# A decoder trunk on one core: a fixed order of work up to the first pair of heads

## The chip, the core and the metric

The kernel runs on one core of a Trainium2 chip. A core has TensorE (matmuls, named PE in the profile, with PEld for the loading of weights into the array), VectorE (DVE), ScalarE (ACT), GpSimd (POOL) and SyncE (SP), whose queue only issues transfers here. Each engine works through its own queue in order, and semaphores hold an instruction until what it needs is there. The metric is the device time of one execution in microseconds (us).

## The reference

The input is 512 tokens of 1024 numbers, in 32 bit. Two layers follow each other: the first mixes tokens by attention with forget gates, the second by a short gated convolution. Each is followed by an MLP with squared ReLU and by a gated per-layer embedding, with an RMSNorm ahead of and behind every part. The change lies in the start of the attention:

```
hn = rmsnorm(x, g[0])
proj = hn @ w_in                      # q, k, v (1024 columns each) and 16 forget logits
q = proj[..., :D] * HEAD_DIM ** -0.5  # 16 heads of 64
log_f = log_sigmoid(proj[..., 3*D:] + b_f)
c = cumsum(log_f, axis=1)             # per head, along the tokens
s = q @ k^T + c[query] - c[key]       # masked: key <= query
o = softmax(s) @ v
```

## The kernel before

**Three products for one.** Every 32-bit operand is kept as a pair, a high part that TensorE takes without loss and the rest. `mm3` (lines 266 to 272) writes a product as three matmuls: high by high, low by high, high by low (lines 268 to 270). `split` (274) makes such a pair: ScalarE casts the high part (276), VectorE subtracts (277). `split_gained` (279) does so for weights that are multiplied by the first norm's gain as well (285 on ScalarE, 287 on VectorE, in halves of 256 columns).

**Weights.** All weights are listed in order of use as tiles of 128 x 512. `fetch(n)` (line 152) issues the loads of tiles up to n on SyncE's queue, into 14 raw buffers (`RAWS`); a raw buffer comes back when its tile is split. `prepare(n)` (175) splits tiles up to n, and fetches what isn't fetched. `wide` and `narrow` ask for one tile, and prepare `soon` tiles more than that one, 8 where nothing else is said (`SOON`). Tiles 0 to 19 are those of v and the forget logits in three blocks of columns (8, 8 and 4 tiles), tiles 20 to 51 those of q and k, four for each pair of heads. All split tiles and most intermediate results live in 70 pages of 128 x 512.

**The attention's start.** The v and logit columns are computed from x before it is normalised; the norm's factor is applied to the result, so TensorE can start at once. `halves` and `part` (472) do the first two blocks of columns, `values(t)` (482) the third, for four blocks of 128 tokens each. `keep_values` (498) applies the factor and splits into pairs. `logs` (419) turns the logits into logarithms. `sums_of_logs` (444) sums them along the tokens on TensorE (448), copies the sum to `c_T` (453) and writes it, less each block's start and negated, to `neg_c` in device memory (457, 461). `normed_x(n, ...)` (718) multiplies half n of x, with features along the partitions, by the factor (728) and splits it into `hT`. q and k are computed from `hT`: `project(i)` (521) does pair i of the heads, k first, then q, in eight steps of three matmuls each. It casts and scales the results, and copies k's parts to the other half of the partitions by four transfers (547). For pair 0 these are issued on ScalarE's queue, for the other pairs on SyncE's. `bias(h)` (550) broadcasts a head's row of `neg_c` to the 128 partitions, in four transfers (562), and GpSimd fills the masked corner of each (563). `scores` (568) is the product of q and k for one head and one block of queries, with the softmax behind it; `turn` transposes the weights and `mix` multiplies them by v.

**What sets the order.** A planner with its own estimate of times orders the instructions of each engine. Within the block that begins at line 733 the instructions of all five engines keep the order in which they are written among themselves; the planner may still place later instructions between them, where it thinks that the engine is free. That block ends at line 793, after `keep_values(1, 3)`. What follows, the last third of v, the two `bias` calls and pair 0, is ordered by the planner. From line 801 on, `main` is a stream of steps of the remaining pairs: eight steps of pair 1's k come first, and after them scores, transposes, products with v and steps of the stream alternate.

Of the kernel before, what the change touches and what calls it, by code (L numbers as in the profile page):

```python
# [8 lines left out]
F32 = mybir.dt.float32  # L9
# [6 lines left out]
P = 128  # L16
D = 1024
S = 512
# [3 lines left out]
KT = D // P  # L22
NB = S // P
# [6 lines left out]
RAWS = 14  # L30
# [38 lines left out]
def trunk(ctx: ExitStack, tc, x, xT, pT, g, gT, wv, wqk, bf, wo, wci, wcq, cw, wco, wup, wdn, wpp, wpg, out):  # L69
# [82 lines left out]
    def fetch(upto):  # L152
        while len(fetched) < min(upto, len(loads)):
            n = len(fetched)
            raw = raws.tile([P, S], F32, tag="raw", name=f"raw{n}")
            fetched.append(raw)
            src = loads[n]
            nc.sync.dma_start(raw[:, : src.shape[-1]], src)
# [16 lines left out]
    def prepare(upto, lows=None):  # L175
        while begun[0] < min(upto, len(order)):
            n = begun[0]
            begun[0] += 1
            key, at = order[n]
            for of in (key[:3], key[:2]):  # L180
                if of in recipes:
                    derive(of)
            hi, lo = page(f"wh{n}", F32R), page(f"wl{n}", F32R)
            if isinstance(at, tuple):
                raw, w = derived.pop(key), S
                eng = nc.gpsimd if (key[0] == "dn" and key[2] > 0) or key[-1] in ON_POOL else nc.vector
            else:
                fetch(at + 1)
                raw, eng, w = fetched[at], lows or nc.vector, loads[at].shape[-1]
                fetched[at] = None  # L190
            if key[0] in ("v", "qk"):
                split_gained(hi, lo, raw, w, key[2], eng, key[0] == "qk" or key[1] == 2)
            else:
                split(hi[:, :w], lo[:, :w], raw[:, :w], eng)
            ready[key] = Pair(hi[:, :w], lo[:, :w])

    def wide(*key, soon=SOON):

        prepare(where[key] + 1 + soon)
        return ready[key]  # L200

    def narrow(*key, k, c, soon=SOON):

        c += k % 2 * 256
        return wide(*key, k // 2, soon=soon).at(lambda u: u[:, c : c + P])
# [206 lines left out]
    def attention(hT, raw_x, b_f, warm, work, by_hand):  # L412
# [31 lines left out]
        def sums_of_logs(tri):  # L444
            ps_c = bank("ps_c")
            for b in range(NB):
                for half in (lf.hi, lf.lo):
                    nc.tensor.matmul(
                        ps_c[:H, b * P :], half[:, b * H : (b + 1) * H], tri[:, : S - b * P],
                        start=b == 0 and half is lf.hi, stop=b == NB - 1 and half is lf.lo,  # L450
                    )
            c_T = page("c_T")
            nc.vector.tensor_copy(c_T[:H, :S], ps_c[:H, :])
            for b in range(NB):
                n = (b + 1) * P
                t = page(f"neg_c{b}")
                nc.vector.tensor_scalar(
                    out=t[:H, :n], in0=c_T[:H, :n], scalar1=c_T[:H, b * P : b * P + 1],
                    scalar2=-1.0, op0=ALU.subtract, op1=ALU.mult,
                )  # L460
                nc.sync.dma_start(neg_c[b, :, :n], t[:H, :n])
# [20 lines left out]
        def values(t):  # L482

            ps = bank(f"v2_{t}")
            for k in range(KT):
                w = wide("v", 2, k // 2).at(lambda u: u[:, k % 2 * 256 : k % 2 * 256 + 256])
                mm3(ps[:, :256], of_x(k, t), w, k == 0, k == KT - 1)
            keep_values(2, t, ps)

# [28 lines left out]

        stacked, probs, outs, both = {}, {}, {}, {}

        def project(i):

            heads = [[page(f"{n}{i}_{e}", F32R) for n in ("qs", "kh", "kl")] for e in range(2)]
            stacked[i] = heads
            for s in (1, 0):
                ps = bank(f"qk{i}_{s}")
                for k in range(KT):
                    mm3(
                        ps, narrow("qk", i, k=k, c=s * P),
                        hT.at(lambda h: h[:, k, :]), k == 0, k == KT - 1,  # L530
                    )
                    if k < KT - 1:
                        yield
                for e in range(2):
                    a, b = slice(64 * e, 64 * e + 64), slice(64 - 64 * e, 128 - 64 * e)
                    q, kh, kl = heads[e]
                    if s == 0:
                        nc.scalar.mul(q[a, :S], ps[a, :], HD**-0.5)
                        nc.vector.scalar_tensor_tensor(
                            out=q[b, :S], in0=ps[a, :], scalar=HD**-0.5,  # L540
                            in1=q[a, :S].bitcast(F32), op0=ALU.mult, op1=ALU.subtract,
                        )
                    else:
                        split(kh[a, :S], kl[a, :S], ps[a, :])
                        for h in (kh, kl):
                            eng = nc.sync if i else nc.scalar
                            eng.dma_start(h[b, :S].bitcast(F32), h[a, :S].bitcast(F32))
                yield

        def bias(h):  # L550
# [167 lines left out]
        def normed_x(n, r_rows):  # L718

            halves = [raw_x[t][n][:, :S].rearrange("p (j c) -> p j c", j=4) for t in range(NB)]  # L720

            def low(t):
                to = lambda u: u[:, 4 * n : 4 * n + 4, t * P : (t + 1) * P]
                split(to(hT.hi), to(hT.lo), halves[t])

            for t, h in enumerate(halves):
                r = r_rows[:, t * P : (t + 1) * P].unsqueeze(1).to_broadcast([P, 4, P])
                nc.vector.tensor_tensor(out=h, in0=h, in1=r, op=ALU.mult)
                if t:
                    low(t - 1)  # L730
            low(NB - 1)

        with tc.manual_schedule(engines={E.PE, E.DVE, E.Activation, E.Pool, E.SP}):
            work(9)
            banks_v = {(0, t): bank(f"v0_{t}") for t in range(NB)}

            def halves(c, *at):
                for t, n in at:
                    if (c, t) not in banks_v:
                        banks_v[c, t] = bank(f"v{c}_{t}")  # L740
                    part(c, banks_v[c, t], t, n)

            split_x(0, 0)
            prepare(4)
            halves(0, (0, 0))
            split_x(0, 1)
            split_x(1, 0)
            halves(0, (1, 0))
            prepare(KT)
            fetch(2 * KT)  # L750
            nc.sync.dma_start(b_f, bf[0:1, :].partition_broadcast(P))
            first_x = [load_x("xc", t) for t in range(NB)]
            fetch(2 * KT + 4)
            halves(0, (0, 1))
            split_x(1, 1)
            halves(0, (1, 1))
            for t in (2, 3):
                for n in range(2):
                    split_x(t, n)
                    halves(0, (t, n))  # L760
            tri, ones = page("tri", F32R), page("ones")
            nc.gpsimd.memset(ones[:, :S], 1.0)
            nc.gpsimd.affine_select(
                out=ones[:, :S], in_=ones[:, :S], compare_op=ALU.is_ge, fill=0.0, base=0,
                pattern=[[1, S]], channel_multiplier=-1,
            )
            nc.vector.tensor_copy(tri[:, :S], ones[:, :S])
            prepare(KT + 4)
            halves(1, (0, 0), (1, 0))
            prepare(2 * KT)  # L770
            halves(1, (0, 1), (1, 1))
            for t in range(NB):
                inverse(t)
            halves(1, (2, 0))
            r_rows = rows()
            halves(1, (2, 1), (3, 0), (3, 1))
            for two in ((0, 1), (2, 3)):
                for t in two:
                    logits(t, banks_v[0, t])
                for t in two:  # L780
                    keep_values(0, t, banks_v[0, t])
                prepare(2 * KT + 4)
            steps = logs()
            next(steps)
            keep_values(1, 0, banks_v[1, 0])
            next(steps)
            keep_values(1, 1, banks_v[1, 1])
            next(steps)
            normed_x(0, r_rows)
            keep_values(1, 2, banks_v[1, 2])  # L790
            sums_of_logs(tri)
            normed_x(1, r_rows)
            keep_values(1, 3, banks_v[1, 3])
        for t in range(NB):
            values(t)
            if t == 1:
                bias(0)
                bias(1)
        for _ in project(0):
            pass  # L800
        main = stream()
        for _ in range(8):
            next(main)
# [513 lines left out]
```

## Time and profile before

| | us |
|---|---|
| median of three runs | 1232.86 (1232.01 to 1233.35) |
| the profiled execution | 1232.7 |
| its span, first to last instruction | 1231.0 |
| busy time of TensorE's matmuls | 1211.1 |
| of VectorE | 928.9 |
| of ScalarE | 691.1 |
| of GpSimd | 653.7 |

The mean granted TensorE clock of the profiled execution is 0.994 of full speed. In a row of a timeline stand the start, the duration, the engine, the line, the operation with out<-in and its count; a bracket at the end gives the idle time before it and what ended it. An engine's name with a q is its queue, and a row there is the issue of a transfer. In a row of waits stand the waiting engine, line and tile, the one it waited for, and then the total in us, how many times, and the longest. Tiles go by the names in the program: raw is a loaded weight tile, wh and wl its pair, v the values, hTh and hTl the pair of normalised x, qk the bank that q or k is summed in, kh and kl the pair of k, qs q with its rest, sc the scores, pr, prr and prl the masks, which become the softmax weights, and pT those transposed.

### The profile page before, as it was taken

The numbers are of one execution on the slowest core, as the hardware profiler recorded it, in microseconds if no ns is written. First come the engines' busy times: TensorE is split into PE (matmuls) and PEld (weight loads), VectorE is DVE, ScalarE is ACT, GpSimd is POOL, SyncE is SP. The second block draws the span as 40 slices with busy tenths as digits, with TensorE's granted clock in tenths as the row PEclk, the third lists the DMA queues.
The fourth block names the chain that finished last, engine by engine and source line by source line (L and its number), as shares of the span: only waits on it lengthen the run. The fifth ranks groups of instructions, "written<-read, shape, count | busy, mean of one in ns | idle before, by whom it ended". The sixth has DMA issues, their size and how long they took to land.

```text
span 1231.0 us, 18748 instructions
## 1 busy us (share of the span) xinstructions
PE 1211.1 (98%) x6175; PEld 1031.8 (84%) x6175; DVE 928.9 (75%) x1474; ACT 691.1 (56%) x1465; POOL 653.7 (53%) x616
## 2 busy tenths in 40 slices
PE   9969999999999999999999999999999999999997
PEld 8858888788888888888889999989888888888886
DVE  6857889667787667869777798866776887669873
ACT  6657778646745644465467443445756345635551
POOL 2025666235876787866213155315677777778310
PEclk9979999999999999999999999999999999999999
DMA  9364554442342234328232133542422443135501
GB/s 314 112 184 147 165 167 133 138 171 65 124 138 94 77 104 137 111 70 288 81 104 86 53 98 100 155 153 97 128 72 75 137 137 95 60 120 169 174 8 61
DMA packets 87314, 150.84 MB, mean 123 GB/s; under 512 B 10352, under 2 KB 18080, under 8 KB 87216
## 3 DMA queue, kind: packets, MB, share of 16 engines
q1 hardware_dynamic: 86320, 148.58, 38.4%
q10 hardware_dynamic: 896, 1.05, 0.3%
q8 instruction: 49, 0.80, 0.3%
q14 instruction: 49, 0.40, 0.1%
HBM read 139.03 MB, written 6.37 MB: 118 GB/s over the span
## 4 chain that ended last, share of the span: by engine, by line
PE 90%; DVE 2%; issue 2%; ACT 2%; DMA 2%; POOL 1%; SPq 0%; POOLq 0%; ACTq 0%; DVEq 0%
PE up L270 9%; PE up L268 9%; PE up L269 9%; PE dn L268 8%; PE dn L270 8%; PE dn L269 8%; PE v L476 3%; PE qk L269 2%; PE qk L270 2%; PE qk L268 2%; PE pg L269 2%; PE pg L268 2%; PE pg L270 2%; PE pT L591 1%; PE co L269 1%
## 5 line engine op out<-in xcount | busy, mean ns | idle before, releaser
L277 DVE TENSOR_TENSOR wl<-raw,wh 128x512 fp32r<-128x512 f32 x346 | 344.2, 1040 | 14.2 <-ACT wh L276 13.4
L269 PE MATMUL up<-hTh,wl 128*128 128x512 f32 (+1 forms) x576 | 210.2, 365 | 0.0
L270 PE MATMUL up<-hTl,wh 128*128 128x512 f32 (+1 forms) x576 | 209.7, 366 | 0.3 <-DVE hTl L277 0.3
L268 PE MATMUL up<-hTh,wh 128*128 128x512 f32 (+1 forms) x576 | 208.7, 366 | 0.0
L276 ACT CAST wh<-raw 128x512 fp32r<-128x512 f32 x346 | 189.4, 625 | 4.5 <-DVE xd L373 4.4
L972 ACT ACTIVATE r<-up 128x512 f32<-128x512 f32 (+1 forms) x72 | 39.5, 548 | 204.0 <-PE up L270 204.0
L277 POOL TENSOR_TENSOR wl<-dn_T,wh 128x512 fp32r<-128x512 f32 x96 | 133.0, 1417 | 30.1 <-ACT wh L276 30.1
L269 PEld LDWEIGHTS up<-hTh,wl 128*128 128x128 f32 x576 | 108.7, 189 | 17.6
L270 PEld LDWEIGHTS up<-hTl,wh 128*128 128x128 f32 x576 | 108.3, 189 | 18.0 <-DVE hTl L277 0.5
L268 PEld LDWEIGHTS up<-hTh,wh 128*128 128x128 f32 x576 | 108.6, 189 | 17.4
L168 POOL TENSOR_TENSOR dn_T<-raw,raw 128x512 f32<-128x512 f32 x56 | 85.7, 1543 | 70.4 <-DMA raw<-in_wdn 55.1
L1018 DVE TENSOR_TENSOR acc<-dn,acc 128x512 f32<-128x512 f32 x168 | 107.4, 680 | 15.2 <-PE dn L270 15.0
L168 POOL TENSOR_TENSOR dn_T<-raw,dn_T 128x512 f32<-128x512 f32 x56 | 91.7, 1638 | 2.2
L276 ACT CAST wh<-dn_T 128x512 fp32r<-128x512 f32 x112 | 61.4, 617 | 11.0 <-POOL dn_T L168 11.0
L277 DVE TENSOR_TENSOR A12l<-q,A12h 128x512 fp32r<-128x512 f32 x28 | 21.8, 779 | 56.0 <-ACT A12h L276 56.0
L1032 POOL TENSOR_TENSOR acc<-acc,acc 128x512 f32<-128x512 f32 x28 | 46.9, 1708 | 9.9 <-DVE acc L1018 9.9
L270 PE MATMUL qk<-hTl,wh 128*128 128x512 f32 x128 | 51.2, 401 | 0.0
L269 PE MATMUL qk<-hTh,wl 128*128 128x512 f32 x128 | 50.8, 398 | 0.4 <-DVE wl L287 0.4
L268 PE MATMUL qk<-hTh,wh 128*128 128x512 f32 x128 | 50.9, 399 | 0.0
L277 DVE TENSOR_TENSOR A11l<-q,A11h 128x256 fp32r<-128x256 f32 x28 | 23.5, 838 | 36.1 <-ACT A11h L276 36.1
L269 PE MATMUL pg<-wh,hTl 128*128 128x512 f32 x128 | 50.5, 394 | 0.0
L268 PE MATMUL pg<-wh,hTh 128*128 128x512 f32 x128 | 50.4, 394 | 0.0
(404 smaller groups left out, 3311.7 us busy)
## 6 DMA issues: line engine op xcount, KB each, us to landing
raw<-in_wup SPq DMA_DIRECT2D x128, 256.0 KB, 3.0
raw<-in_wdn SPq DMA_DIRECT2D x128, 256.0 KB, 2.8
raw<-in_wcq SPq DMA_DIRECT2D x36, 256.0 KB, 2.8
raw<-in_wqk SPq DMA_DIRECT2D x32, 256.0 KB, 5.3
raw<-in_wpg SPq DMA_DIRECT2D x32, 256.0 KB, 4.4
g<-in_g SPq DMA_DIRECT2D x22, 256.0 KB, 5.4
prl<-neg_c SPq DMA_DIRECT2D x16, 256.0 KB, 6.4
raw<-in_wo SPq DMA_DIRECT2D x16, 256.0 KB, 4.5
```

The source lines that it names most:

```text
L168: ins = nc.gpsimd.tensor_tensor(out=B[name], in0=B[a], in1=B[b], op=op)
L268: nc.tensor.matmul(ps, a.hi, b.hi, start=start, stop=False)
L269: nc.tensor.matmul(ps, a.lo, b.hi, start=False, stop=False)
L270: nc.tensor.matmul(ps, a.hi, b.lo, start=False, stop=stop)
L276: nc.scalar.copy(hi, src)
L277: return eng.tensor_tensor(out=lo, in0=src, in1=hi.bitcast(F32), op=ALU.subtract)
L476: nc.tensor.matmul(ps[:, : V_CHUNKS[c][1]], getattr(of_x(k, t), p), getattr(ready["v", c, k], of), start=k == 0 and p == of, stop=k == KT ...
L591: nc.tensor.transpose(ps[:, b * P : (b + 1) * P], probs[h][b][:, j * P : (j + 1) * P], ident)
L972: nc.scalar.activation(r[:, :n], ps[:, :n], AF.Relu)
L1018: ins = nc.vector.tensor_tensor(out=a, in0=banks[s], in1=a, op=ALU.add)
L1032: nc.gpsimd.tensor_tensor(out=a, in0=a, in1=acc[i, s][:, :S], op=ALU.add)
```

## The change

The block with the written order is extended to the end of pair 0's q and k. In it:

- one fetch goes further (to tile 22 instead of 20), and two are added (to tile 30 and tile 34);
- `sums_of_logs`, and behind it both `bias` calls, stand between the two halves of normalised x, ahead of the values of token block 2;
- weight tiles 20 and 21 are prepared ahead of the second half of normalised x, tiles 22 and 23 behind it, and the four of pair 1 after pair 0's k is complete;
- `values` and `project(0)` are called inside the block, and ask for no tile beyond the one they use;
- all four copies of pair 0's k are issued on SyncE's queue.

```diff
-                w = wide("v", 2, k // 2).at(lambda u: u[:, k % 2 * 256 : k % 2 * 256 + 256])
+                w = wide("v", 2, k // 2, soon=0).at(lambda u: u[:, k % 2 * 256 : k % 2 * 256 + 256])
...
-        def project(i):
+        def project(i, soon=SOON):
...
-                        ps, narrow("qk", i, k=k, c=s * P),
+                        ps, narrow("qk", i, k=k, c=s * P, soon=soon),
...
-                            eng = nc.sync if i else nc.scalar
-                            eng.dma_start(h[b, :S].bitcast(F32), h[a, :S].bitcast(F32))
+                            nc.sync.dma_start(h[b, :S].bitcast(F32), h[a, :S].bitcast(F32))
...
-            fetch(2 * KT + 4)
+            fetch(RAWS + KT)
...
             prepare(2 * KT)
+            fetch(RAWS + 2 * KT)
             halves(1, (0, 1), (1, 1))
...
             keep_values(1, 1, banks_v[1, 1])
             next(steps)
+            fetch(RAWS + 2 * KT + 4)
             normed_x(0, r_rows)
+            sums_of_logs(tri)
+            bias(0)
+            bias(1)
             keep_values(1, 2, banks_v[1, 2])
-            sums_of_logs(tri)
+            prepare(2 * KT + 6)
             normed_x(1, r_rows)
+            prepare(2 * KT + 8)
             keep_values(1, 3, banks_v[1, 3])
-        for t in range(NB):
-            values(t)
-            if t == 1:
-                bias(0)
-                bias(1)
-        for _ in project(0):
-            pass
+            for t in range(NB):
+                values(t)
+            for n, _ in enumerate(project(0, 0)):
+                if n == KT - 1:
+                    prepare(2 * KT + 12)
         main = stream()
```

## The prediction

> **What bounds the kernel now.** I read the page first, then TensorE's waits, then busy time by stretch, then the queues of the stretch that stood out. The page: matmuls fill 1211.1 of 1231.0 us, so TensorE is the bound nearly everywhere, and about 20 us of idle time are all that a change of order can win, apart from a slower clock.
>
> ```profile
> span 1231.0 us, 18748 instructions
> PE 1211.1 (98%) x6175; PEld 1031.8 (84%) x6175; DVE 928.9 (75%) x1474; ACT 691.1 (56%) x1465; POOL 653.7 (53%) x616
> ```
>
> The waits of TensorE (total, times, longest, in us) say where most of that idle time is: two waits, once each, at the first scores, for copies of kh and kl.
>
> ```profile
> PE sc L575 <- DMA kh<-kh: 7.5, 1, 7.5
> PE sc L576 <- DMA kl<-kl: 2.2, 1, 2.2
> PE warm_p L1188 <- DVE warm L1170: 1.5, 1, 1.5
> PE qk L269 <- DVE wl L287: 0.4, 1, 0.4
> PE pT L591 <- DVE pl L596: 0.4, 1, 0.4
> ```
>
> Busy time by stretch (length, then each engine's busy us, granted clock, DMA share, GB/s). The cuts are the starts and ends of TensorE's idle times: it is full to 73.13, empty to 80.62, all but empty to 83.30, then full at half clock to 89.44.
>
> ```profile
> 41.32:46.55 5.23, 5.23 (x35) 4.41 (x34) 5.05 (x9) 3.19 (x8) 0.00 (x0) 1.00 0.01 3
> 46.55:56.00 9.45, 9.45 (x82) 9.43 (x81) 8.54 (x21) 4.45 (x12) 0.00 (x0) 1.00 0.04 10
> 56.00:73.13 17.13, 16.77 (x74) 13.26 (x72) 12.71 (x36) 11.46 (x32) 1.55 (x5) 1.00 0.57 162
> 73.13:80.62 7.49, 0.00 (x1) 0.03 (x1) 1.38 (x2) 1.65 (x3) 1.03 (x4) 0.68 0.96 259
> 80.62:83.30 2.68, 0.45 (x2) 0.26 (x2) 0.69 (x1) 2.64 (x6) 0.00 (x0) 0.50 0.43 108
> 83.30:89.44 6.14, 6.14 (x16) 5.08 (x17) 5.34 (x19) 4.67 (x13) 1.59 (x3) 0.50 0.45 136
> 89.44:100.00 10.56, 10.56 (x51) 8.74 (x50) 6.18 (x20) 6.59 (x17) 7.64 (x11) 0.99 0.50 145
> 100.00:220.00 120.00, 119.31 (x653) 101.43 (x652) 103.68 (x303) 95.37 (x247) 76.91 (x106) 1.00 0.52 152
> ```
>
> Why the copies are late, in two queues. SyncE first (start, us): the masks' source neg_c is written at 48.95, but six weight loads stand ahead of the eight broadcasts, which go out only from 62.50 on, the last just before 68.90. The six loads each need a raw buffer back, and the first comes back when VectorE starts on the weights at 56.45 (below).
>
> ```profile
> 30.09 3.68 SPq L158 DMA_DIRECT2D raw<-in_wqk  x6
> 48.95 2.10 SPq L461 DMA_DIRECT2D neg_c<-neg_c  x4
> 57.35 5.05 SPq L158 DMA_DIRECT2D raw<-in_wqk  x6
> 62.50 0.39 SPq L562 DMA_DIRECT2D prr<-neg_c  x1
> ...
> 68.90 19.27 SPq L158 DMA_DIRECT2D raw<-in_wqk  x10
> ```
>
> Then ScalarE, which itself issues the four copies of pair 0. The first half of k is rounded at 66.85, its copy goes out only at 74.09, and the second half, next in ScalarE's order, starts at 77.67 after 10.21 us without work that the profile puts down to a broadcast still under way. Everything behind, q's scaling too, is as late.
>
> ```profile
> 66.85 0.61 ACT L276 CAST kh<-qk 64x512 fp32r<-64x512 f32 x1
> 74.09 0.52 ACTq L547 DMA_DIRECT2D kh<-kh  x1
> 77.67 0.58 ACT L276 CAST kh<-qk 64x512 fp32r<-64x512 f32 x1 [10.21 <-DMA prl<-neg_c]
> 80.14 0.59 ACT L538 ACTIVATE qs<-qk 64x512 fp32r<-64x512 f32 x1 [0.75 <-DVE qs L539]
> ```
>
> **The change part by part.** No arithmetic is added or taken away; instructions are put in a fixed order on all five engines as far as pair 0's q and k, and four copies change queue. So I lay the new order out with the durations of VectorE, which does most there, and of TensorE.
>
> ```profile
> 41.18 0.23 DVE L277 TENSOR_TENSOR lf_l<-logf,lf_h 128x64 fp32r<-128x64 f32 x1 [0.37 <-ACT lf_h L276]
> 47.95 0.67 DVE L453 COPY c_T<-ps_c 16x512 f32<-16x512 f32 x1
> 48.65 1.26 DVE L457 TENSOR_SCALAR neg_c<-c_T 16x128 f32<-16x128 f32 x4
> 55.41 1.13 DVE L514 SCALAR_TENSOR_TENSOR v<-v,n_r,v 128x128 fp32r<-128x128 f32 x4 [0.35 <-ACT v L512]
> 56.45 6.42 DVE L287 SCALAR_TENSOR_TENSOR wl<-raw,first_g,wh 128x256 fp32r<-128x256 f32 x16
> 62.80 2.14 DVE L514 SCALAR_TENSOR_TENSOR v<-v,n_r,v 128x128 fp32r<-128x128 f32 x8
> 68.03 0.67 DVE L277 TENSOR_TENSOR kl<-qk,kh 64x512 fp32r<-64x512 f32 x1
> 80.77 0.69 DVE L539 SCALAR_TENSOR_TENSOR qs<-qk,qs 64x512 fp32r<-64x512 f32 x1 [0.66 <-ACT qs L538]
> ```
>
> And TensorE's first matmuls of the sums of logs, of q and k, and of the transposes:
>
> ```profile
> 43.30 0.40 PE L448 MATMUL ps_c<-tri,lf_h 128*16 128x512 f32 x1
> 56.00 0.63 PE L268 MATMUL qk<-hTh,wh 128*128 128x512 f32 x2
> 97.61 0.27 PE L591 MATMUL pT<-ident,prr 128*128 128x128 f32 x1
> ```
>
> (1) Earlier fetches: in the old queue too all loads that 14 raw buffers allow by then have gone out by 33.8 (the row at 30.09), so the fetches written out by hand cost and win nothing; behind them the queue issues nothing until 48.95.
>
> (2) TensorE from the sums of logs on: the same matmuls as between the rows at 43.30 and 56.00, only with the sums in one piece. Its logs are ready at 41.4, so it reaches k of pair 0 at 56.0 as before.
>
> (3) VectorE, laid end to end: first half of normalised x until 46.55 (the first cut); c_T and neg_c 0.67 + 1.26, to 48.4; the values of block 2 1.13, to 49.5; two weight tiles, four operations of 6.42/16 = 0.40, 1.6, to 51.1; second half of x, which I take to last the 5.23 of the first, to 56.3; two more tiles, to 57.9; values of block 3, to 59.0; last third of the values 2.14, to 61.2. TensorE's 72 matmuls of the third stretch take 16.77/72 = 0.233 each. It wants the second half of x and weight tile 22 at the fifth step of k, 56.0 + 12 x 0.233 = 58.8, tile 23 at 60.2. They are there at 56.3, 57.1 and 57.9. The margin is 1.7 us or more, so the 0.36 us wait for the first weight (in the 0.4 of the waits) goes and none comes in its place. ScalarE has less to do in each step and goes ahead of it.
>
> (4) k is complete at 61.6, q at 67.2, the eight steps of pair 1's k at 72.8. Casting kh takes 0.61 and kl 0.67, one half after the other: the halves are ready by 62.9 and 64.2. Then VectorE makes pair 1's four tiles (3.2 us) to 67.4; the first is there at 65.0 and wanted at 67.2. q's two halves follow at 67.2 + 2 x (0.59 + 0.69) = 69.8.
>
> (5) Copies and broadcasts. The broadcasts now wait in SyncE's queue for neg_c to land, and behind them stand only the copies. GpSimd's eight mask fills move with them; it has no work from 41.32 to 56.00, so nothing stands behind those. Issue to landing, by kind:
>
> ```profile
> neg_c<-neg_c SPq DMA_DIRECT2D x1, 32.0 KB, 1.7
> kh<-kh SPq DMA_DIRECT2D x14, 128.0 KB, 3.9
> kh<-kh ACTq DMA_DIRECT2D x2, 128.0 KB, 5.8
> prl<-neg_c SPq DMA_DIRECT2D x16, 256.0 KB, 6.4
> ```
>
> The last neg_c goes out by about 49.6 and lands at 51.3; the broadcasts, at the 0.39 of the row at 62.50, are issued by about 54.5, and the last lands about 60, ahead of the copies. The copies go out at 62.4 to 65; at 3.9 us the first half's are there by 67.4, at 5.8 by 69.4. q is the later input, and both come before 72.8, where the first scores stand in TensorE's order. So the 7.49 us wait goes, and of the next stretch 2.68 - 0.45 = 2.23. With ScalarE no longer issuing copies, its 10.21 us hole goes, which matters only through these two waits.
>
> (6) The clock. At half clock TensorE did 0.45 + 6.14 us of work; at full clock that takes half, 3.3 us less. The row shows full clock up to the gap and 0.50 behind it, so with no gap I take all of it. The ends are 0, if the clock falls anyhow, and 3.3. The Trainium skill ("TensorE: Matmul & The Clock Gate", Part 1: The HAM clock gate) says that the array falls to half rate after an idle window of about 3.4 us and is back after about 3.4 us of sustained work. By that figure only some 1.7 us would come back here, an estimate from the page, and the time would be 1221.4. The trace disagrees on the length: 6.59 us of busy time lay at 0.50, and the sum goes by it.
>
> (7) What is late next: VectorE. Its work of 41.32 to 100.00 is 39.9 us (the seven rows' sum). Without the gap it has 58.68 - 13.4 = 45.3 us for it, 88%. In 100 to 220 it sustains 103.68/120 = 86% beside a full TensorE. At 86% it would need 46.2, 0.9 us more; the first place to show that is the first transposes (97.61 in the old order). Ends 0 and 0.9; I take 0.45.
>
> Sum: 7.49 + 2.23 + 0.36 + 3.3 - 0.45 = 12.9 saved. The profiled execution took 1232.7, its span 1231.0 and 1.7 around it; 1232.7 - 12.9 = 1219.8. That execution lies 0.16 under the median of the runs, too little to shift the number.
>
> **The rivals.**
>
> A, part of the wait stays. The planner still places the later weight loads, and may put some ahead of the copies in SyncE's queue. A load for raws that come back with pair 1's tiles (67.4) would let the copies out at 68 and land them at 72 to 74, which costs about 1 us. For raws of the four tiles after (70.6, by 3.2 us more), the copies land at 75 to 77: a wait of 2 to 4 us, and a gap brings the half clock: the mean of 0.68 over 7.49 us is 2.7 us at full and the rest at half, so a wait over some 2.7 us costs up to 3.3 more. 1222 to 1227. For it: the old queue did the like with the broadcasts. Against: by the layout those raws come back after the copies are ready.
>
> B, slower: the copies stand behind loads that wait for VectorE work which itself comes after the scores. The old queue shows ten such loads from 68.90 for 19.27 us, to 88.2. Copies behind them land at 92; the first scores, complete to go at 83.30 before, would be 8.8 us later, and the half clock is paid as before: 1241. It decides where the copies go out later than about 79. For it: SyncE works in order, and pair 0's copies were not in that queue before. The Trainium skill ("DMA: Bandwidth & Descriptors", Anatomy of one DMA) says that DMA engines don't wait on semaphores, and that the wait is in the issuing sequencer before dispatch. The row of 19.27 us for ten issues agrees with that.
>
> C, no change: the scores wait for something else of the same length, the half clock included, such as weights that VectorE makes ahead of the first maxima. By (7) the load says no; it would be 1232.
>
> D, the planner orders everything behind by its own times, and a shift there may open waits. All other waits of TensorE behind the start are 0.4 us or less in total (the list goes by length), so I hold a loss over 3 us unlikely; with A's, 1222 to 1227.
>
> **How the numbers follow.** Forecast 0.73, its own range 1218 to 1222 (all bounds of (6) apart from 0, and (7)); A and D together 0.12; C 0.04; B 0.11. Faster by over 0.2%, about what a measurement can tell here, is 0.73 + 0.12; the range goes up to A's 1227 and down to 1217, a microsecond for small waits that may go too.
>
> **What would show it.** Right: no wait for kh or kl at the first scores; broadcasts issued by 55, copies by 66, from SyncE; ScalarE's 10.21 us hole gone; clock 1.0 throughout from 60 to 100; the first transposes about 13 us sooner. Wrong: SyncE's copies behind a long run of weight loads; TensorE waiting at k's fifth step for x or a weight; a new wait at the first transposes of over 1 us; or the half clock without a gap.

## The result, and the profile after

The changed kernel takes 1219.57 us (median of 4 runs, 1218.23 to 1221.29) beside 1232.43 of the kernel before: a ratio of 0.9898, 95% interval 0.9879 to 0.9917. Run twice more beside other kernels, it gave 0.9899 (0.9884 to 0.9914) and 0.9903 (0.9888 to 0.9917). That is 12.9, 12.5 and 11.6 us less by the medians, where 12.9 was forecast.

The page of the changed kernel gives the span and the share of each engine:

```profile
span 1216.5 us, 18743 instructions
PE 1205.5 (99%) x6175; PEld 1027.5 (84%) x6175; DVE 931.4 (77%) x1474; ACT 691.4 (57%) x1465; POOL 655.4 (54%) x616
```

Its longest waits of TensorE (waiting engine, line and tile, what it waited for, then total, times, longest in us):

```profile
PE warm_p L1191 <- DVE warm L1173: 1.5, 1, 1.5
PE ps_o L613 <- ACT ph L594: 1.2, 1, 1.2
```

Both waits for copies are gone, and one new wait of 1.2 us stands behind them. At the cuts of the prediction (length, then the busy us of TensorE, its weight loads, VectorE, ScalarE and GpSimd, granted clock, DMA share, GB/s):

```profile
56.00:73.13 17.13, 17.13 (x79) 14.30 (x78) 14.43 (x39) 13.98 (x37) 1.77 (x6) 1.00 0.87 239
73.13:80.62 7.49, 7.49 (x36) 6.27 (x36) 5.91 (x20) 6.38 (x16) 3.36 (x4) 1.00 0.77 235
...
83.30:89.44 6.14, 4.98 (x28) 4.07 (x27) 5.98 (x18) 5.79 (x17) 4.53 (x8) 1.00 0.59 162
```

TensorE is full where it stood still, the clock is 1.00, and 6.14 - 4.98 = 1.16 us are missing in one place. The timeline of SyncE's queue (start, us; the first row is that of the first broadcast):

```profile
48.42 0.36 SPq L561 DMA_DIRECT2D prr<-neg_c  x1
...
52.84 0.79 SPq L561 DMA_DIRECT2D prl<-neg_c  x1
53.73 5.83 SPq L158 DMA_DIRECT2D raw<-in_wqk  x4
60.92 0.53 SPq L546 DMA_DIRECT2D kh<-kh  x1
...
63.02 1.24 SPq L546 DMA_DIRECT2D kl<-kl  x1
64.34 12.64 SPq L158 DMA_DIRECT2D raw<-in_wqk  x12
```

The timeline of ScalarE:

```profile
60.31 0.58 ACT L276 CAST kh<-qk 64x512 fp32r<-64x512 f32 x1 [1.39 <-PE qk L270]
...
65.75 0.59 ACT L538 ACTIVATE qs<-qk 64x512 fp32r<-64x512 f32 x1 [0.19 <-PE qk L270]
...
72.64 1.28 ACT L581 ACT_TABLE_LOAD   x1
...
85.72 0.89 ACT L285 ACTIVATE wh<-raw,first_g 128x256 fp32r<-128x256 f32 x2
86.64 0.59 ACT L594 CAST ph<-pT 128x512 fp32r<-128x512 f32 x1
```

The broadcasts go out from 48.42 to 53.63, ahead of the weight loads, and the copies from 60.92 to 64.26, ahead of the next twelve. ScalarE now waits for k's product (1.39 us) and not for a transfer. So the chain from k to the first scores is as laid out. TensorE's timeline, at its first scores, transposes and product with v:

```profile
71.00 0.22 PE L574 MATMUL sc<-kh,qs 128*128 128x128 f32 x1
...
82.44 0.27 PE L590 MATMUL pT<-ident,prr 128*128 128x128 f32 x1
...
87.27 0.50 PE L613 MATMUL ps_o<-ph,v 128*128 128x512 f32 x1 [1.16 <-ACT ph L594]
```

Where the 14.5 us between the two spans lie, from the starts of these stages in the two timelines (from k to the first product with v the stages hold the same 72, 55 and 22 matmuls in both kernels):

| from, to | before | after | less by |
|---|---|---|---|
| start to the sums of logs | 43.30 | 41.91 | 1.4 |
| to k of pair 0 | 12.70 | 12.74 | 0.0 |
| to the first scores | 24.62 | 16.35 | 8.3 |
| to the first transposes | 16.99 | 11.44 | 5.6 |
| to the first product with v | 3.42 | 4.83 | -1.4 |
| to the end | 1129.97 | 1129.23 | 0.7 |

The first row is not to be put down to the change. It lies before 12 us, where TensorE's matmuls stand in the same order in both kernels. One row of TensorE's timeline before, then the one that answers to it after (four matmuls in each):

```profile
9.33 1.11 PE L476 MATMUL v<-wh,xh 128*128 128x272 f32 x4
```

```profile
8.69 0.66 PE L476 MATMUL v<-wh,xh 128*128 128x272 f32 x4
```

The same matmuls run for some 3.5 us at little more than half speed in the one, and at full speed in the other. The traces' own records of the granted clock tell why: full clock is first granted at 11.04 us in the kernel before and at 5.52 in the changed kernel. (Ahead of the first record the tables of busy time print 1.00.) In two more profiles of the changed kernel it comes at 6.45 and 6.88, so the moment isn't fixed by the kernel alone. Of thirteen profiled executions, six show three or more rows near 1.11 us here. In four, the kernel before among them, the first grant comes between 10.66 and 11.04; in the other two (copies alone on SyncE, filled gap) it comes at 5.20 and 4.47, and the clock is at 0.50 again for 3.41 us, from 8.61 and 7.88 on. A comparison of two profiles can be off by 1.4 us for this reason, so times of two profiles are compared below from the start of the sums of logs on where it matters (43.30 before, 41.91 after). The profiled execution after is also the fastest of its four, 1.3 us below their median. So the difference of the medians, 12.9, is to be taken rather than 14.5.

### The profile page after: what moved, and what is told of

Its sections match the earlier page's. It is cut to its first block, busy times and chain, and to the rows that moved or that the text cites. A ratio compares the mean times of both kernels' runs of the same rounds, so it can differ in the third digit from the quotient of the medians.

```text
span 1216.5 us, 18743 instructions
## 1 busy us (share of the span) xinstructions
PE 1205.5 (99%) x6175; PEld 1027.5 (84%) x6175; DVE 931.4 (77%) x1474; ACT 691.4 (57%) x1465; POOL 655.4 (54%) x616
## 4 chain that ended last, share of the span: by engine, by line
PE 91%; ACT 3%; issue 2%; DVE 2%; POOL 1%; DMA 0%; SPq 0%; POOLq 0%; DVEq 0%; ACTq 0%
PE up L269 9%; PE up L270 9%; PE up L268 9%; PE dn L268 8%; PE dn L270 8%; PE dn L269 8%; PE v L476 3%; PE pg L269 2%; PE pg L268 2%; PE pg L270 2%; PE qk L270 2%; PE qk L269 2%; PE qk L268 2%; PE pT L590 1%; PE co L269 1%
```

## The experiments

### Only the copies change queue

```diff
-                            eng = nc.sync if i else nc.scalar
-                            eng.dma_start(h[b, :S].bitcast(F32), h[a, :S].bitcast(F32))
+                            nc.sync.dma_start(h[b, :S].bitcast(F32), h[a, :S].bitcast(F32))
```

> The kernel before with one edit: pair 0's four copies are issued on SyncE's queue instead of ScalarE's. In its written queue the first copy now stands behind the six loads, the eight broadcasts and five more loads. Theory (broadcasts late, and ScalarE blocked by its own copies): ScalarE is free, casts and q's scaling are done by about 70, copies go out at about 73 and land at about 78.5, so TensorE waits some 5.5 us instead of 9.7 and the half clock stays: about 1228. Rival 1 (the change of queue is the whole gain): 1220. Rival 2 (mechanism B of the prediction: the copies end up behind all the loads): 1241.

Measured: 1231.94, ratio 1.0006 (0.9996 to 1.0015): nothing. TensorE waits 9.3 + 0.8 us instead of 7.5 + 2.2. Its row among the waits:

```profile
PE sc L574 <- DMA kh<-kh: 9.3, 1, 9.3
```

SyncE's queue in the timeline:

```profile
67.79 6.60 SPq L158 DMA_DIRECT2D raw<-in_wqk  x5
74.48 0.53 SPq L546 DMA_DIRECT2D kh<-kh  x1
```

And from the list of transfers issued from 66 to 84 us (KB each, median us from issue to landing):

```profile
kh<-kh SPq DMA_DIRECT2D x2, 128.0 KB, 7.2
```

ScalarE is free as expected, but the copies stand behind five loads. These go out back to back and take until 74.39: they don't wait for a buffer, their issues last 0.5 to 2.9 us each. Then the copies need 6.2 to 7.7 us to land, where they needed 4.9 to 6.4 from ScalarE's queue. No theory had the number; the mechanism is that of rivals A and B, the copies behind loads in SyncE's order, and what it costs is about what the freed ScalarE saves.

### The copies back on ScalarE, the rest changed

```diff
-                            nc.sync.dma_start(h[b, :S].bitcast(F32), h[a, :S].bitcast(F32))
+                            eng = nc.sync if i else nc.scalar
+                            eng.dma_start(h[b, :S].bitcast(F32), h[a, :S].bitcast(F32))
```

> The changed kernel with the queue of pair 0's copies undone: they are issued on ScalarE again. Theory: what blocked ScalarE was a broadcast still under way; in the changed kernel the last broadcast lands at about 62.7, when the copies are about to go out, so at most 1.5 us of it shows on ScalarE and none on TensorE, which comes to the first scores at 71: 1219.6, within 1 us of the changed kernel. Rival (the queue carries the gain): the wait for kh and kl comes back, 1226 or more.

Measured: 1224.19, ratio 0.9941 (0.9926 to 0.9956), some 5 us over the changed kernel by the two ratios. The theory was right on the first scores, which come at 71.35 without a wait, and wrong on the time. ScalarE's timeline:

```profile
62.51 0.58 ACT L276 CAST kh<-qk 64x512 fp32r<-64x512 f32 x1 [1.26 <-DVE kl L277]
...
64.37 3.31 ACT L285 ACTIVATE wh<-raw,first_g 128x256 fp32r<-128x256 f32 x8 [1.27 <-DVE kl L277]
67.70 0.59 ACT L538 ACTIVATE qs<-qk 64x512 fp32r<-64x512 f32 x1
```

TensorE's largest new wait in its timeline:

```profile
90.05 0.72 PE L614 MATMUL ps_o<-ph,v 128*128 128x512 f32 x1 [2.23 <-ACT ph L595]
```

The stretch behind it, cut where the clock changes:

```profile
90.16:93.57 3.41, 3.41 (x9) 2.83 (x10) 2.87 (x9) 2.56 (x9) 3.41 (x5) 0.50 0.50 157
```

Issuing the copies of kl, ScalarE waits for VectorE's kl, twice 1.3 us. From the sums of logs on (42.27 here), q's scaling starts 1.6 us later than in the changed kernel. The first exponential isn't later, because ScalarE has four weight operations less ahead of it; those behind it are up to 1.0 us later, and the cast ahead of the first product with v 2.4 us. TensorE waits 1.1 us at a later score and 2.2 us at the first product with v. Behind this wait the clock is at 0.50 for 3.41 us, which loses another 1.7. So a queue that must not wait matters even where no transfer is late.

### The broadcasts late, behind the copies

```diff
             sums_of_logs(tri)
-            bias(0)
-            bias(1)
...
                     prepare(2 * KT + 12)
+                    fetch(RAWS + 2 * KT + 12)
+                    bias(0)
+                    bias(1)
```

> The changed kernel with the two broadcasts calls moved behind pair 0's k, its copies and the weights of pair 1, and eight more loads put ahead of them: the broadcasts go out at about 67 to 71 instead of 48 to 54, but the copies go out first. Theory: the masks themselves are wanted only when the first maxima are taken (72 to 78), so late broadcasts cost 0 to 2 us through the softmax and no wait at the first scores: 1219.6 to 1222. Rival (broadcasts that late are what the old wait was made of): a wait of several us at the first transposes or scores and the half clock, 1226 or more.

Measured: 1227.49, ratio 0.9967 (0.9954 to 0.9979): 8 us over the changed kernel, and no wait at the first scores. Where it is lost, TensorE's transposes in the timeline:

```profile
85.23 0.33 PE L590 MATMUL pT<-ident,prr 128*128 128x128 f32 x1 [2.13 <-POOL prr L583]
86.14 0.48 PE L590 MATMUL pT<-ident,pr 128*128 128x128 f32 x1 [0.57 <-POOL pr L583]
87.36 0.48 PE L590 MATMUL pT<-ident,prr 128*128 128x128 f32 x1 [0.74 <-POOL prr L583]
```

The stretch behind the first of them, cut by time:

```profile
86.00:92.60 6.60, 5.72 (x15) 4.26 (x16) 2.39 (x6) 4.27 (x10) 5.55 (x6) 0.50 0.78 205
```

GpSimd's last mask fill and its first scaling of softmax weights in the timeline:

```profile
84.30 0.29 POOL L562 TENSOR_SCALAR_AFFINE_SELECT prl<-prl 128x128 f32<-128x128 f32 x1 [0.44 <-DMA prl<-neg_c]
84.57 0.60 POOL L583 TENSOR_SCALAR prr<-prr,rs 128x128 f32<-128x128 f32 x1
```

The same scaling in the changed kernel:

```profile
74.73 0.61 POOL L583 TENSOR_SCALAR prr<-prr,rs 128x128 f32<-128x128 f32 x1 [11.69 <-DVE rs L582]
```

The theory named the right place, the softmax, and left out GpSimd's order. From the sums of logs on (43.10 here), prl's exponential is only 1.1 us later than in the changed kernel. But GpSimd has the mask fills of both heads ahead of its first scaling of softmax weights, and the last of them waits for its broadcast until 84.30. The scaling, whose factor VectorE had ready at 76.46, starts 8.7 us later than in the changed kernel. TensorE waits 3.4 us at the transposes and 1.5 at the first product with v, which comes 7.0 us later, and 5.72 us of work at a clock of 0.50 add 2.9 of these.

### The gap filled with idle matmuls

```diff
         for _ in range(8):
             next(main)
+        fill = bank("fill")
+        for _ in range(40):
+            nc.tensor.matmul(fill, hT.hi[:, 0, :P], hT.hi[:, 0, :], start=True, stop=True)
```

> The kernel before with 40 matmuls whose result nobody reads put between pair 1's k and the first scores. They fill the idle time of TensorE (9.1 us at 0.227 each) and take nothing away from it, so the waits for the copies stay where they were. It prices the half clock alone. Theory: 6.14 us of work behind 83.3 at half clock become 3.1, so 1232.4 - 3.1 = 1229.3. Rival 1 (the page's 3.4 us of half clock): 1.7 less, 1230.7. Rival 2 (the clock falls there anyhow): 1232.4.

Measured: 1235.79, ratio 1.0036 (1.0022 to 1.0050): slower. All three theories missed. The clock is 1.00 through the first scores, as intended. But TensorE then stands at the transposes, as its timeline shows:

```profile
72.88 9.23 PE L806 MATMUL fill<-hTh 128*128 128x512 f32 x40
82.10 0.30 PE L575 MATMUL sc<-kh,qs 128*128 128x128 f32 x1
...
96.04 0.33 PE L591 MATMUL pT<-ident,prr 128*128 128x128 f32 x1 [1.35 <-POOL prr L584]
...
100.53 0.48 PE L591 MATMUL pT<-ident,prl 128*128 128x128 f32 x1 [0.80 <-POOL prl L584]
```

The kernel before reached its first transpose at 97.61 without a wait, at half clock most of the way. With the clock kept, TensorE is there at 96.04 - 1.35 = 94.69 and waits 4.2 us in four pieces; behind them the clock falls after all, to 0.50 from 100.05 to 103.46. The wait need not be the clock's doing: the planner takes the filling for real time and orders what follows anew. On GpSimd it puts three mask fills of the next pair ahead of the first scaling of softmax weights:

```profile
91.86 0.29 POOL L563 TENSOR_SCALAR_AFFINE_SELECT prr<-prr 128x128 f32<-128x128 f32 x1 [14.63 <-DMA prr<-neg_c]
...
95.38 0.60 POOL L584 TENSOR_SCALAR prr<-prr,rs 128x128 f32<-128x128 f32 x1
```

In the kernel before, the last of the first head's four scalings:

```profile
91.11 1.57 POOL L584 TENSOR_SCALAR prl<-prl,rs 128x512 f32<-128x512 f32 x1 [0.48 <-DVE rs L583]
```

The first scaling starts at 95.38 instead of 85.98. The planner also puts two casts of pair 1 ahead of the first exponential (87.12 instead of 84.26), and the filling lasts to 82.10, 1.5 us beyond the old start of the scores. In the kernel before, the first head's weights were all scaled by 92.68, 2.0 us ahead of 94.69: had the order stayed, they would have been ready for the first transposes. So the run doesn't price the half clock, and no run here does so alone. What it shows is that idle matmuls aren't free where a planner counts them, as it then orders the work of the other engines differently.

### q and k ordered by the planner again

```diff
-            for t in range(NB):
-                values(t)
-            for n, _ in enumerate(project(0, 0)):
-                if n == KT - 1:
-                    prepare(2 * KT + 12)
+        for t in range(NB):
+            values(t)
+        for n, _ in enumerate(project(0, 0)):
+            if n == KT - 1:
+                prepare(2 * KT + 12)
```

> The changed kernel with the last third of v and pair 0's q and k taken out of the block with the written order again (they still ask for no further tile, and pair 1's four tiles still come behind k). Theory (the gain is in the broadcasts, the copies' queue and the weights of pair 0 being early, all of which stay): TensorE reaches the first scores within 0.5 us of the changed kernel, and the time is within 1 us of it. Rival (the fixed order itself is what wins): a wait of several us for kh and kl comes back, 1225 or more.

Measured: 1226.51, ratio 0.9960 (0.9948 to 0.9973). The rival has the time; its reason, a wait for kh and kl, isn't there. The theory fails at its first number: from the sums of logs on (42.40 here), the first scores come 4.4 us later than in the changed kernel. The third block of v isn't to blame, as k and q begin 12.7 us behind the sums in both. But the planner lets k and q take turns on TensorE: k is complete at 65.7, 0.4 us ahead of the end of both. (The rows don't tell the two apart; that it is turns, and not q first, is read from ScalarE, whose first work behind its wait is k's cast.) ScalarE's first cast of k in the timeline:

```profile
65.75 0.58 ACT L276 CAST kh<-qk 64x512 fp32r<-64x512 f32 x1 [6.02 <-PE qk L270]
```

TensorE's wait for a weight:

```profile
68.24 0.50 PE L268 MATMUL qk<-hTh,wh 128*128 128x512 f32 x1 [2.08 <-ACT wh L285]
```

The two stretches at half clock, cut where the clock changes:

```profile
69.39:72.80 3.41, 3.41 (x10) 2.62 (x9) 2.97 (x7) 2.56 (x6) 0.00 (x0) 0.50 0.88 234
93.28:100.11 6.83, 6.15 (x16) 4.89 (x17) 5.67 (x16) 5.32 (x15) 4.73 (x7) 0.50 0.64 190
```

k is complete only with q, ScalarE stands 6.02 us, and the weights of pair 1, which come behind k, are late for TensorE, which has nothing else: 2.08 us, then 3.41 us at half clock, then another 2.2 us at the first product with v, where the clock falls a second time, for 6.83 us. The 9.6 us of work in the two stretches lose 4.8.

### q first, in the fixed order

```diff
-            for s in (1, 0):
+            for s in ((0, 1) if i == 0 else (1, 0)):
```

> The changed kernel with one part of the order turned round: of pair 0, q's product comes first and k's second. Theory (k first matters because its halves still have a cast, a copy of 4 to 6 us and the scores ahead of them, while q has only its scaling): k is complete at about 66 instead of 60.3, the copies go out from 66.5 on and land at 72 to 74, TensorE comes to the first scores at 71 and waits 1 to 3 us for kh or kl; the softmax chain is as much later, and a wait of 2 us is enough for the half clock (as seen where the planner ordered q and k): 1222 to 1225. Rival (there is room enough, the margin of q over the copies was some us): no wait at the first scores, 1219.

Measured: 1220.02 beside 1219.86 of the changed kernel on the same chip, ratios 0.9907 (0.9890 to 0.9923) and 0.9903: no difference. The rival holds. The copies go out at 66.31 to 68.76, and the planner, which may still order what comes behind, put the products with kh ahead of those with kl, which start at 73.12 without a wait. The copies land in 3.9 to 4.2 us here, the last at 72.9. So that k comes first is worth nothing that the times can tell; that the two don't take turns is what is left of the fixed order's gain, by the run before, and no run tests it alone.

### Pair 0's weights not ahead

```diff
-            prepare(2 * KT + 6)
             normed_x(1, r_rows)
-            prepare(2 * KT + 8)
```

> The changed kernel without the four weight tiles of pair 0 prepared between the halves of normalised x: each is prepared where k asks for it. Theory by the layout of VectorE: the first tile then comes behind the values, at about 57, and TensorE, ready for k at about 55, waits 2 to 2.5 us; behind that VectorE makes half a tile in 0.41 us against 0.68 of TensorE's steps, so no further wait: 2 to 3 us over the changed kernel, and up to 3 more if the clock falls. Rival (weights sooner win nothing, ScalarE and VectorE have idle time for them anyway): no wait at k, the same time as the changed kernel.

Measured: 1222.53, ratio 0.9931 (0.9918 to 0.9943), 3.6 us over the changed kernel's median on that chip. TensorE's timeline at k:

```profile
56.75 0.50 PE L268 MATMUL qk<-hTh,wh 128*128 128x512 f32 x1 [1.53 <-ACT wh L285]
57.91 0.50 PE L269 MATMUL qk<-hTh,wl 128*128 128x512 f32 x1 [0.66 <-DVE wl L287]
```

In place as forecast, but in two pieces, 2.2 us together, where the theory had one and nothing behind it. From the sums of logs to the first scores the profile is 2.7 us longer than the changed kernel's, and equal behind that; the mean clock of that execution stays at 0.999. The median has 3.6, above the 2 to 3 of the theory. The profiled execution is the fastest of its five, 1221.38, and where the others lose more isn't shown.

### The exponential's table loaded early

```diff
             prepare(2 * KT + 6)
+            nc.scalar.activation(stat("f_w", n_f), logit, AF.Exp)
```

> The changed kernel with one small exponential added on ScalarE behind the first two weight tiles, so that the table of 1.28 us is loaded in ScalarE's idle time at about 48 instead of at 72.6, ahead of the first softmax. Its result isn't used. Theory (behind the first scores the chain of the softmax over VectorE, ScalarE and GpSimd ends last, which makes the wait of 1.16 us at the first product with v): the chain comes 1.28 us sooner, that wait goes, 1.2 us below the changed kernel. Rival (that wait comes from the weights that ScalarE does ahead of the cast, wherever the table is loaded): the wait stays within 0.3 us, and so does the time.

> The kernel with the early table again, beside the changed kernel on the same chip, for its size: 0.7 to 1.2 us below it, and again no wait at the first product with v.

Measured: 1218.02 and 1218.07, ratios 0.9892 (0.9878 to 0.9905) and 0.9891 (0.9876 to 0.9906). On the two chips its mean of four runs lies 1.0 and 1.4 us below that of the changed kernel. Both together are 1.2 us less, give or take 0.8 (95%, from the scatter of the sixteen runs). In the timeline of the second of these runs, ScalarE's load in its new place:

```profile
47.85 1.28 ACT L796 ACT_TABLE_LOAD   x1
```

And TensorE's first product with v, which no longer waits:

```profile
87.55 0.50 PE L613 MATMUL ps_o<-ph,v 128*128 128x512 f32 x1
```

So the wait of 1.16 us was the softmax chain's, as the theory had it, and this version beats both kernels. The second run's size, 1.4 by means and 1.8 by medians, lies above the 0.7 to 1.2 expected for it. The runs of the changed kernel beside them came out nearly as expected, 1218.98 and 1219.86, each with its wait of 1.16 us.

> The changed kernel once more, on the same chip as the three runs beside it, as their base: 1219 to 1220, and again one wait of about 1.2 us at the first product with v, since that is in the written and planned order and not in the chance of one execution.

> The changed kernel as base of the other two: 1219, with its wait of 1.2 us at the first product with v.

## Why the prediction was right, point by point

The sum was right: 12.9 us forecast, 12.9, 12.5 and 11.6 measured. That the first agrees to the tenth is luck, as (7) below was too small and the rest of the profile made up for it. The terms:

- **The waits for the copies, 7.49 + 2.23, and 0.36 at the first weight.** To the first scores the stage is 8.3 us shorter (7.49 + 0.36 = 7.85 forecast; the rest is that a matmul's modelled end overlaps the next one's start). From there to the first transposes it is 5.6 shorter, against 2.23 + 3.3 = 5.5 with the clock of (6).
- **(3) and (4), the layout of VectorE and TensorE.** The first tiles were ready in time, k was complete at 60.3 and the first scores began at 71.0, which with the 1.4 us of the start is 61.7 and 72.4 against 61.6 and 72.8. Without the early weights TensorE waits 2.2 us at k: they are what step (3) took them for.
- **(5), copies and broadcasts.** With the same 1.4 us, broadcasts were out by 55.0 (54.5 forecast) and copies by 65.7 (65). The landing was sized too small: the copies took 6.9 to 7.4 us, not 3.9 to 5.8. The last landed at 69.9, 1.1 us ahead of the first scores, where the forecast left 3.4 us. So the wait went with little to spare. What the prediction didn't say is that neither part alone gives the whole: the queue without the order is worth nothing, the order without the queue 7 of the 12 us, late broadcasts with early copies 4.
- **(6), the clock.** The stage with the 3.3 us came out as forecast (5.6 for 5.5), with the same 55 matmuls in both kernels and the clock at 1.00. The wait of 2.23 and the clock went together, and no run parts them. The step found the trace at odds with 3.4 us for the way up. Cut by the clock's records it isn't: the low clock lasted 13.65 us, four times 3.41, and TensorE stood idle for 3.41, 2.97, 0.58 and 0 us in the four parts. The 6.59 us of work in them, on which the sum rested, were read rightly.
- **(7), what is late next.** A wait of 1.16 us, just over the bound of 0.9; with it the stage to the first product with v is 1.4 us longer, where 0.45 was taken. The step named VectorE and the first transposes. It was ScalarE ahead of a cast, and the first product with v. The early table takes the wait away, so the table (72.64) is one cause; that the weight at 85.72 is another is only argued.
- **Rival A** held that a wait under some 2.7 us leaves the clock alone. 2.08 us were enough where the planner ordered q and k, and 2.23 with the copies on ScalarE. The mean of 0.68 over one gap gave the time from the gap's begin to the fall, and not the shortest gap that makes the clock fall.
- **Rival B** is real as a mechanism: in the kernel with only the queue changed, copies stand behind five loads until 74.39. It ended level rather than slower. In the changed kernel the planner placed the four loads of 53.73 ahead of the copies, and they were out by 59.6, 1.4 us before the first copy.

The sums in the expectations went wrong more than the prediction did, mostly in one way: they asked whether a wait at one place goes or comes. They left out that the softmax has no room ahead of the first product with v, where the changed kernel already waits 1.16 us, and that an engine which waits in its order, ScalarE for kl or GpSimd for a broadcast, holds up all that stands behind.

## What to carry to other kernels

When a long wait is taken out, every chain that ran beside it loses the same time, so work out the next one before counting the gain. Here the softmax was next, 1.16 us too late, and changes that brought the first product with v 2.4 and 7.0 us later (copies on ScalarE, late broadcasts) cost 5 and 8 us. An instruction that issues a transfer on a computing engine holds up that engine for whatever the transfer must wait for (twice 1.3 us on ScalarE), and on a queue of its own it stands behind the loads ahead of it (five of them, 6.60 us): ask both before moving it. The same holds for a computing instruction that waits for a transfer: GpSimd's mask fills held up work that had been ready for 8 us. And a stall of TensorE of some 2 us can cost nearly as much again in clock: 2.08 us here, then 3.41 us at half speed, which lose 1.7.

## What the runs showed of the hardware that was not expected

- The records of the granted clock in the thirteen traces follow a fixed step: every stretch at 0.50 that lies between two at full clock lasted 3.41 us or a whole multiple of it (3.41, 6.83, 10.24 and 13.65). Counted in windows of 3.41 us from the first record on, and behind the first 12 us, the clock fell in every window of full clock in which TensorE stood idle for 2.00 us or more, and in none with 1.72 or less. So a wait of 2.08 us brought 3.41 us at 0.50, as it lay in one window, and waits of 1.53 and 0.66 us close together left the clock at full, as the edge of a window lay between them. In the first 12 us this doesn't hold: two runs lost the clock behind windows with 0.98 us idle.
- The Trainium skill ("TensorE: Matmul & The Clock Gate", Part 1: The HAM clock gate) gives 3.4 us for the way down and for the way up, in a window that runs freely. The length of the window agrees. For the way down the traces show less: 2.00 us of idle time in it were enough.
- Full clock was first granted between 4.47 and 11.04 us, though the first matmul starts at 1.50 in all thirteen traces. What sets the moment is open.
- A copy of 128 KB within the core took anything from 2.2 us from issue to landing (pair 0's, where the planner ordered q and k) to 7.7 (with the copies alone on SyncE), on the same queue. What sets it is open; in the changed kernel it was 6.9 to 7.4.
